# A decoder kernel: where the value projection's second weight block is fetched, where one accumulated pair is issued, and where the first keys are split

## The chip, the cores and the metric

The kernel runs on one core of a Trainium2 chip. The metric is the device time of one execution in microseconds. TensorE (PE in the profile) multiplies, ACT and DVE (ScalarE and VectorE) work on tiles in SBUF and PSUM, POOL (GpSimd) does small arithmetic and issues accumulating DMAs, and SP, ACT and POOL each issue DMAs on a queue of their own.

## What is computed

A two-layer decoder over 512 tokens of width 1024: a gated linear attention layer with its MLP, then a layer of stick-breaking attention with its MLP. Each mixer and each MLP is followed by a layer norm of the residual sum. The part that matters here is the seam between the layers:

```python
        h = layer_norm(DEEPNORM_ALPHA * h + sq_relu_mlp(h, mlp_w_up[layer], mlp_w_down[layer]),
                       ln_g[layer, 1], ln_b[layer, 1])
...
                kv = h @ kv_w
                k_sh = kv[..., :D].reshape(B, S, SB_HEADS, SB_HEAD_DIM)
                v_sh = kv[..., D:].reshape(B, S, SB_HEADS, SB_HEAD_DIM)
            q = (h @ sb_w_q[j]).reshape(B, S, SB_HEADS, SB_HEAD_DIM)
```

The norm of the first layer's MLP gives h (512 x 1024); keys, values and queries are products of h with 1024 x 1024 weights.

## The kernel before

**Numbers in two parts.** Every float32 operand of a product is split into a high part in float32r, which ACT copies (`hi`, L70 for weights, L98 for activations), and the remainder, which DVE subtracts (`lo`, L72 and L99). A product is three matmuls: hi by hi, hi by lo, lo by hi. Weights come in tiles of 128 x 1024 float32, 512 KB. A weight tile is fetched either through a pool of three tiles called `raw` on SP's queue (`split_piece`, L64), or into one of eight block tiles called `B`. The `hi` and `lo` tiles have pools of six. A tile of a pool is given out again in turn, and the instruction that fills it waits until the last reader of its former contents is done.

**Four token tiles.** h is held as four tiles of 128 tokens, 0 to 3. When the MLP has added its last product to a tile (DVE, L169), the two statistics instructions (L177) and their aggregate (L182) run on DVE, the factor on POOL (L183, L184), and DVE centres and scales the tile (L190). PE then turns the tile by eight 128 x 128 transposes (L231, a "turn"), ACT applies the norm's gain and bias while it copies out of PSUM (L234, into the tiles `s`), and L98 and L99 split the result into the tiles `T`: for each half u of the 1024 columns a hi (T_4181, T_4183) and a lo tile (T_4182, T_4184). `finish` (L245) does this as the MLP's last steps come; the turns of tiles 2 and 3 are left over as `late` and are called inside `values`.

**Values by seven products.** `values` (L768) computes V = h Wv by Strassen-Winograd's scheme on 2 x 2 blocks: the tokens split into tiles 0, 1 and 2, 3, the inner dimension into two halves, the columns of V into two halves. `v_weights(k, h, j)` is half h (256 rows) of weight block (k, j). Some operands are sums of weight blocks. These are formed in the block tiles, partly by accumulating DMAs on POOL's queue (`more`, L762), partly by DVE (L821, L822). `load` (L752) fetches plain blocks on ACT's queue (L758).

The order of PE's work in this stage is written out in `values`: the first product (`p1`, weights (0,0), plain) on tile 0; the turn of tile 2; the first product on tile 1; the second (`p2`, weights (1,0), plain) on tile 0; the turn of tile 3; the second on tile 1; the first pair's keys in two halves of 256 tokens (`cols_by`, 24 matmuls each), the first half of which needs only tiles 0 and 1; the first pair's queries (24 matmuls of 512 columns); then the fourth, fifth, sixth, third and seventh product. Each product is 24 matmuls of 512 columns (L794). The first and second product need only tiles 0 and 1.

Within an engine the instructions run in order, and that order is settled when the program is built: a scheduler places them by its own estimate of readiness, and `tc.keep_in_program_order` pins those that are given to it. A DMA that waits holds up what stands behind it in its engine's order; so does a split that waits for its weights.

The fetches of the stage before the change: `p1` and `p2` (four raw tiles), the keys' and queries' weights (one raw tile each) on SP's queue, in that order, so that with three raw tiles the second half of `p2` waits until the first half of `p1` is split. On ACT's queue `load` fetches blocks (1,1) and (0,1) when the norm of tile 0 begins, and (0,0) and (1,0) behind the turn of tile 1. On POOL's queue `more` adds (0,1) to the first and (0,0) to the second of these, two DMAs each, when the norm of tile 1 has begun (after `yield t` for t = 1).

## Time and profile before

| what | us |
|---|---|
| median of 3 runs | 1126.36 |
| lowest and highest | 1123.74 and 1127.30 |
| the profiled execution, whole | 1127.99 |
| its span, first to last instruction | 1126.3 |
| the stage that the change edits, on PE | 546.25 to 609.2 of the span |

The profile is of one execution, and its rows are times from the start of the span. The page cuts the span into 40 slices of 28.2 us; one of its rows is the clock that PE was granted, in tenths of full speed (9 is 90% or more):

```profile
PEclk9999999999999999999989999999999999999999
```

The one slice with an 8 begins at 563. The rows of the timeline show start and duration of an instruction (or of several alike, with their count), its engine, line and operation, the tiles it writes and reads, and in brackets how long the engine had been idle and what it waited for. Matmuls overlap in these rows, so their pace is read from the distance of their starts.

### The profile page before, as it was taken

The numbers are of one execution on the slowest core, as the hardware profiler recorded it, in microseconds if no ns is written. First come the engines' busy times: TensorE is split into PE (matmuls) and PEld (weight loads), VectorE is DVE, ScalarE is ACT, GpSimd is POOL, SyncE is SP. The second block draws the span as 40 slices with busy tenths as digits, with TensorE's granted clock in tenths as the row PEclk, the third lists the DMA queues.
The fourth block names the chain that finished last, engine by engine and source line by source line (L and its number), as shares of the span: only waits on it lengthen the run. The fifth ranks groups of instructions, "written<-read, shape, count | busy, mean of one in ns | idle before, by whom it ended". The sixth has DMA issues, their size and how long they took to land.

```text
span 1126.3 us, 14423 instructions
## 1 busy us (share of the span) xinstructions
PE 1111.5 (99%) x5515; PEld 920.9 (82%) x5515; DVE 828.5 (74%) x993; ACT 559.9 (50%) x839; POOL 175.0 (16%) x217
## 2 busy tenths in 40 slices
PE   9999999999999999999899999999999999999998
PEld 7888888898888888888778777788988888888886
DVE  4578649958957856849688898896479767667677
ACT  4455437643534533535565666654445435336353
POOL 1011222200100100121300335240100000000232
PEclk9999999999999999999989999999999999999999
DMA  7441399492670760877924321211946815816783
GB/s 242 126 131 56 120 248 210 130 302 77 203 208 19 204 187 23 228 180 163 247 58 125 100 89 62 76 38 38 273 139 180 253 54 150 223 38 183 176 135 87
DMA packets 108089, 162.78 MB, mean 145 GB/s; under 512 B 12466, under 2 KB 37426, under 8 KB 108020
## 3 DMA queue, kind: packets, MB, share of 16 engines
q1 hardware_dynamic: 86228, 119.39, 32.7%
q0 software_dynamic: 19328, 37.75, 19.4%
q10 hardware_dynamic: 2464, 4.72, 1.1%
q8 instruction: 43, 0.70, 0.2%
q14 instruction: 26, 0.21, 0.1%
HBM read 158.69 MB, written 3.15 MB: 144 GB/s over the span
## 4 chain that ended last, share of the span: by engine, by line
PE 95%; DVE 2%; DMA 1%; ACT 1%; issue 1%; POOL 0%; SPq 0%; POOLq 0%; ACTq 0%; DVEq 0%
PE ps L355 28%; PE ps L93 19%; PE ps L95 19%; PE ps L94 19%; PE ps L794 3%; PE ps L976 2%; PE ps L925 2%; PE ps L962 2%; PE ps L231 1%; DMA raw<-in_kv_w_dram 1%; DVE lo L72 1%; DMA h<-in_x_dram 0%; PE ps L584 0%; PE ps L121 0%; PE ps L649 0%
## 5 line engine op out<-in xcount | busy, mean ns | idle before, releaser
L355 PE MATMUL ps<-hi,T 128*128 128x512 f32 x1008 | 313.4, 390 | 0.1
L93 PE MATMUL ps<-T,hi 128*128 128x512 f32 (+1 forms) x776 | 291.7, 376 | 1.8 <-ACT hi L70 1.8
L95 PE MATMUL ps<-T,lo 128*128 128x512 f32 (+1 forms) x776 | 288.2, 371 | 0.9 <-DVE lo L72 0.9
L94 PE MATMUL ps<-T,hi 128*128 128x512 f32 (+1 forms) x776 | 288.2, 371 | 0.0
L72 DVE TENSOR_TENSOR lo<-raw,hi 128x1024 fp32r<-128x1024 f32 x132 | 160.8, 1223 | 97.5 <-ACT hi L70 93.9
L355 PEld LDWEIGHTS ps<-hi,T 128*128 128x128 f32 x1008 | 188.9, 188 | 40.0 <-DVE T L99 0.6
L70 ACT ACTIVATE hi<-raw 128x1024 fp32r<-128x1024 f32 x132 | 139.8, 1064 | 164.3 <-PE ps L94 53.5
L70 ACT ACTIVATE hi<-B 128x1024 fp32r<-128x1024 f32 x116 | 122.3, 1058 | 172.5 <-PE ps L94 103.8
L72 DVE TENSOR_TENSOR lo<-B,hi 128x1024 fp32r<-128x1024 f32 x116 | 140.4, 1220 | 85.4 <-ACT hi L70 85.2
L355 PE MATMUL ps<-lo,T 128*128 128x512 f32 x504 | 196.1, 389 | 0.0
L93 PEld LDWEIGHTS ps<-T,hi 128*128 128x128 f32 x776 | 147.6, 190 | 26.4 <-ACT hi L70 2.2
L95 PEld LDWEIGHTS ps<-T,lo 128*128 128x128 f32 x776 | 147.6, 190 | 26.2 <-DVE lo L72 1.2
L94 PEld LDWEIGHTS ps<-T,hi 128*128 128x128 f32 x776 | 147.6, 190 | 23.3
L314 POOL DMA_DIRECT2D B<-in_mlp_w_down_dram x52 | 62.9, 1257 | 543.9 <-DMA B<-in_mlp_w_down_dram 411.2
L355 PEld LDWEIGHTS ps<-lo,T 128*128 128x128 f32 x504 | 94.6, 188 | 19.6
L169 DVE TENSOR_TENSOR h<-h,ps 128x512 f32<-128x512 f32 x110 | 74.7, 681 | 6.9 <-PE ps L95 4.0
L93 PE MATMUL ps<-hi,T 128*128 128x512 f32 x192 | 77.4, 403 | 0.0
L95 PE MATMUL ps<-hi,T 128*128 128x512 f32 x192 | 75.3, 392 | 0.0
L94 PE MATMUL ps<-lo,T 128*128 128x512 f32 x192 | 75.1, 391 | 0.0
L99 DVE TENSOR_TENSOR T<-s,T 128x1024 fp32r<-128x1024 f32 (+1 forms) x50 | 53.4, 1070 | 20.8 <-ACT T L98 20.8
L952 DVE TENSOR_TENSOR_SCAN r<-r,begin 128x512 f32<-128x512 f32 x40 | 65.8, 1651 | 2.8 <-ACT r L949 2.8
L953 POOL TENSOR_TENSOR w<-w,r 128x512 f32<-128x512 f32 x32 | 52.2, 1632 | 94.3 <-DVE r L952 68.2
(190 smaller groups left out, 1246.0 us busy)
## 6 DMA issues: line engine op xcount, KB each, us to landing
raw<-in_mlp_w_up_dram SPq DMA_DIRECT2D x64, 512.0 KB, 5.8
B<-in_mlp_w_down_dram SPq DMA_DIRECT2D x64, 512.0 KB, 5.4
B<-in_mlp_w_down_dram POOLq DMA_DIRECT2D x52, 512.0 KB, 8.0
raw<-in_gla_w_in_dram SPq DMA_DIRECT2D x20, 512.0 KB, 3.7
raw<-in_mlp_w_down_dram SPq DMA_DIRECT2D x16, 512.0 KB, 4.5
B<-in_gla_w_o_dram POOLq DMA_DIRECT2D x14, 512.0 KB, 9.6
raw<-in_kv_w_dram SPq DMA_DIRECT2D x14, 512.0 KB, 5.2
B<-in_gla_w_o_dram SPq DMA_DIRECT2D x8, 512.0 KB, 6.1
```

The costliest lines, as they stand in the source:

```text
L70: nc.scalar.activation(hi, raw, AF.Copy)
L72: nc.vector.tensor_tensor(lo, raw, hi.bitcast(F32), op=ALU.subtract)
L93: keep(nc.tensor.matmul(ps, lhsT=a[0], rhs=b[0], start=first, stop=False))
L94: keep(nc.tensor.matmul(ps, lhsT=a[0], rhs=b[1], start=False, stop=False))
L95: keep(nc.tensor.matmul(ps, lhsT=a[1], rhs=b[0], start=False, stop=last))
L99: keep(nc.vector.tensor_tensor(lo, ps, hi.bitcast(F32), op=ALU.subtract))
L169: nc.vector.tensor_tensor(h, h, ps, op=op)
L314: nc.gpsimd.dma_start(out=b.rearrange("p (a b) -> p a b", a=2), in_=weights(k, h, j), accum_op=ALU.add)
L355: nc.tensor.matmul(banks[s], lhsT=a(k, s)[x], rhs=b[k][y], start=opens and (k, x, y) == (0, 0, 0), stop=closes and (k, x, y) == (3, 1, 0), ...
L794: nc.tensor.matmul(banks[s], lhsT=a(k, s)[x], rhs=b[k][w], start=opens and (k, x, w) == (0, 0, 0), stop=closes and (k, x, w) == (3, 1, 0), ...
L952: nc.vector.tensor_tensor_scan(down, down, begins[kind][:, ::-1], 1.0, op0=ALU.mult, op1=ALU.max)
L953: (nc.vector if kind == 2 else nc.gpsimd).tensor_tensor(w, w, r[:, 1:S + 1], op=ALU.mult)
```

## The change

- The first four block loads on ACT's queue are now (1,0) and (1,1) in place of (1,1) and (0,1); the later four are (0,0) and (0,1) in place of (0,0) and (1,0).
- The second product takes its weights from block (1,0) itself, split where it lies (`pieces(b21)`), in place of a plain fetch through two raw tiles. The same block later takes its sums and serves the fourth product, as before.
- POOL adds (0,1) to block (1,1) when the norm of tile 1 has begun, as before. Its other pair, now (0,0) added to block (0,1), is issued in `values`, behind the norms of tiles 2 and 3.
- The keys' weights are fetched and split (`piece_128`) in the code ahead of the turn of tile 3 in place of behind the second product.
- The splits of the fourth product's weights are pinned to program order.

```diff
-    def split_tile(raw, a):
+    def split_tile(raw, a, keep=lambda ins: ins):
...
-        nc.scalar.activation(hi, raw, AF.Copy)
+        keep(nc.scalar.activation(hi, raw, AF.Copy))
...
-        nc.vector.tensor_tensor(lo, raw, hi.bitcast(F32), op=ALU.subtract)
+        keep(nc.vector.tensor_tensor(lo, raw, hi.bitcast(F32), op=ALU.subtract))
...
-        b22, b12, b11, b21 = bs
-        p1, p2 = plain(0, 0), plain(1, 0)
+        b21, b22, b11, b12 = bs
+        p1, p2 = plain(0, 0), pieces(b21)
         part(0, whole(0, 0), p1, ys, True, False)
         late.pop(0)(None)
         part(1, whole(0, 0), p1, ys, True, False)
         part(0, whole(1, 0), p2, xs)
+        keys0 = piece_128(kv_w, 0)
         late.pop(0)(None)
         part(1, whole(1, 0), p2, xs)
-        keys0 = piece_128(kv_w, 0)
+        more(b12, 0, 0)
...
-        p4 = pieces(b21)
+        p4 = pieces(b21, tc.keep_in_program_order)
...
                 if t == 0:
-                    bs.extend(load(pool, k, j) for k, j in ((1, 1), (0, 1)))
+                    bs.extend(load(pool, k, j) for k, j in ((1, 0), (1, 1)))
                 yield t
+                if t == 1:
+                    more(bs[1], 0, 1)
                 if t == ~1:
-                    bs.extend(load(pool, k, j) for k, j in ((0, 0), (1, 0)))
-                if t == 1:
-                    more(bs[0], 0, 1)
-                    more(bs[1], 0, 0)
+                    bs.extend(load(pool, k, j) for k, j in ((0, 0), (0, 1)))
```

Three places in the engines' orders show what moves. The first is on ACT, at the end of the turn of tile 1. `hi_4611` of before and `hi_4605` of the change are the second half of the second product's weights; T_4181 is the hi of the turned tokens' first 512 columns. Before:

```order
L234 ACTIVATE s_4185<-ps_4530,bcol_4188,gcol_4187 128x128 x3
L70 ACTIVATE hi_4611<-raw_4609 128x1024
L98 ACTIVATE T_4181<-s_4185 128x4x128
L758 DMA B_4541<-in_kv_w_dram 128x2x512
L758 DMA B_4543<-in_kv_w_dram 128x2x512
```

And with the change:

```order
L234 ACTIVATE s_4185<-ps_4528,bcol_4188,gcol_4187 128x128 x3
L70 ACTIVATE hi_4605<-B_4429 128x1024
L98 ACTIVATE T_4181<-s_4185 128x4x128
L758 DMA B_4539<-in_kv_w_dram 128x2x512
L758 DMA B_4541<-in_kv_w_dram 128x2x512
```

The order is the same; what the split reads has moved from a raw tile to a block tile. The second place is on ACT too, from the end of the turn of tile 2 on. `hi_4713` of before and `hi_4672` of the change are the keys' weights, `hi_4769` and `hi_4765` the queries'. Before:

```order
L234 ACTIVATE s_4185<-ps_4639,bcol_4188,gcol_4187 128x128 x3
L234 ACTIVATE s_4186<-ps_4676,bcol_4188,gcol_4187 128x128
L98 ACTIVATE T_4181<-s_4185 128x4x128
L234 ACTIVATE s_4186<-ps_4676,bcol_4188,gcol_4187 128x128 x3
L234 ACTIVATE s_4185<-ps_4687,bcol_4188,gcol_4187 128x128
L98 ACTIVATE T_4183<-s_4186 128x4x128
L234 ACTIVATE s_4185<-ps_4687,bcol_4188,gcol_4187 128x128 x3
L70 ACTIVATE hi_4713<-raw_4711 128x1024
L98 ACTIVATE T_4181<-s_4185 128x4x128
L70 ACTIVATE hi_4769<-raw_4767 128x1024
L98 ACTIVATE T_4812<-s_4186 128x4x256
```

And with the change:

```order
L234 ACTIVATE s_4185<-ps_4633,bcol_4188,gcol_4187 128x128 x3
L70 ACTIVATE hi_4672<-raw_4670 128x1024
L98 ACTIVATE T_4181<-s_4185 128x4x128
L234 ACTIVATE s_4186<-ps_4676,bcol_4188,gcol_4187 128x128 x4
L234 ACTIVATE s_4185<-ps_4687,bcol_4188,gcol_4187 128x128
L98 ACTIVATE T_4183<-s_4186 128x4x128
L234 ACTIVATE s_4185<-ps_4687,bcol_4188,gcol_4187 128x128 x3
L70 ACTIVATE hi_4765<-raw_4763 128x1024
L98 ACTIVATE T_4181<-s_4185 128x4x128
L98 ACTIVATE T_4808<-s_4186 128x4x256
```

The keys' split has moved from behind the turn of tile 3 to the end of the turn of tile 2, and the queries' split stands one T further ahead, in the keys' old place. DVE's two subtractions (L72) move with them. The third place is on POOL, around the norms of tiles 2 and 3; ve and rs are their factors. One piece of the difference, - before and + with the change:

```order
 L184 TENSOR_TENSOR rs_4458<-ve_4457,mhalf 128x1
-L765 DMA B_4427<-in_kv_w_dram 128x2x512
-L765 DMA B_4429<-in_kv_w_dram 128x2x512
 L765 DMA B_4431<-in_kv_w_dram 128x2x512
 L765 DMA B_4433<-in_kv_w_dram 128x2x512
-L183 TENSOR_SCALAR ve_4564<-mv_4563 128x1
-L184 TENSOR_TENSOR rs_4565<-ve_4564,mhalf 128x1
-L183 TENSOR_SCALAR ve_4585<-mv_4584 128x1
-L184 TENSOR_TENSOR rs_4586<-ve_4585,mhalf 128x1
+L183 TENSOR_SCALAR ve_4562<-mv_4561 128x1
+L184 TENSOR_TENSOR rs_4563<-ve_4562,mhalf 128x1
+L183 TENSOR_SCALAR ve_4583<-mv_4582 128x1
+L184 TENSOR_TENSOR rs_4584<-ve_4583,mhalf 128x1
+L765 DMA B_4543<-in_kv_w_dram 128x2x512
+L765 DMA B_4545<-in_kv_w_dram 128x2x512
```

Of the four accumulating DMAs ahead of the norms of tiles 2 and 3 two remain, and the other pair stands behind them. On SP's queue the two fetches for the second product are gone, and the fetches behind them move up. On PE the order changes by one row: the first matmul of the queries stands behind the first matmul of the keys' second half.

## The prediction

> **What bounds the kernel now.** I read the page first, then what TensorE waits for, then the clock it was granted around those waits, and only then the engines it waited for.

> ```profile
> PE 1111.5 (99%) x5515; PEld 920.9 (82%) x5515; DVE 828.5 (74%) x993; ACT 559.9 (50%) x839; POOL 175.0 (16%) x217
> ```

> PE is busy for 99% of the span, so a change that leaves the matmuls alone can win only PE's idle time, and time in which PE is busy at a lower clock. The table of PE's waits (engine, line, what was waited for, total us, times, longest) says where the idle time is:

> ```profile
> PE ps L231 <- DVE h L190: 4.3, 2, 4.2
> PE ps L93 <- ACT hi L70: 1.8, 1, 1.8
> PE ps L95 <- DVE lo L72: 0.9, 1, 0.9
> ```

> PE's rows in order of time put all three into the stage that the change edits, between the last matmul of the layer's MLP and the fourth of the seven products:

> ```profile
> 546.25 0.39 PE L794 MATMUL ps<-hi,T 128*128 128x512 f32 x1
> 548.74 0.39 PE L794 MATMUL ps<-hi,T 128*128 128x512 f32 x1
> 553.32 1.60 PE L231 MATMUL ps<-ident,h 128*128 128x128 f32 x8 [4.19 <-DVE h L190]
> 561.36 1.04 PE L231 MATMUL ps<-ident,h 128*128 128x128 f32 x8
> 562.15 0.48 PE L794 MATMUL ps<-hi,T 128*128 128x512 f32 x1
> 566.93 0.38 PE L93 MATMUL ps<-T,hi 128*128 128x256 f32 x1 [1.80 <-ACT hi L70]
> 568.38 0.58 PE L95 MATMUL ps<-T,lo 128*128 128x256 f32 x1 [0.95 <-DVE lo L72]
> 574.40 0.28 PE L93 MATMUL ps<-T,hi 128*128 128x256 f32 x1
> 576.56 0.40 PE L93 MATMUL ps<-T,hi 128*128 128x512 f32 x1
> 582.03 0.39 PE L794 MATMUL ps<-hi,T 128*128 128x512 f32 x1
> ...
> 582.19 27.20 PE ps L794 x120
> ```

> What the stage would take without waits follows from its own undisturbed rows: 120 matmuls of 512 columns take 27.20, so 0.227 each; eight transposes take 562.15 - 561.36 = 0.79; the 18 of 256 columns from 574.40 to 576.56 take 0.12 each; the 24 of the queries run from 576.56 to 582.03, 5.47. The stage has 48 at 0.227 (10.9), two turns (1.6), 48 at 0.12 (5.8) and 5.5, which is 23.7 us. It takes 582.03 - 546.25 = 35.8. So **12.1 us** are lost, and only 6.9 of them are the three waits. The granted clock shows where the rest is (stretch, its length, PE busy and count, clock, DMA share, GB/s):

> ```profile
> 546.93:550.35 3.42, 2.20 (x10) 1.00 1.11 212
> 550.35:553.76 3.41, 0.44 (x4) 1.00 1.12 215
> 553.76:557.17 3.41, 3.41 (x12) 0.50 1.09 276
> ...
> 564.00:567.41 3.41, 1.61 (x7) 1.00 0.23 61
> 567.41:570.83 3.42, 2.47 (x12) 0.50 0.61 123
> 570.83:574.24 3.41, 3.41 (x18) 0.50 0.64 190
> 574.24:577.65 3.41, 3.41 (x26) 1.00 0.01 2
> ```

> After the stretch with 0.44 busy the clock is half for 3.41; after the one with 1.61 busy it is half for 6.83. Half of the first is 1.7, half of the second without its 0.95 of idle is 2.9: 4.6 us are slow clock, and the remaining half microsecond is pipelines that drain and fill.

> **The first wait.** ACT, then DVE, then POOL:

> ```profile
> 540.73 8.83 DMA raw<-in_kv_w_dram
> ...
> 544.85 1.22 ACT L234 ACTIVATE s<-ps,bcol,gcol 128x128 f32<-128x128 f32 x3
> 549.64 1.06 ACT L70 ACTIVATE hi<-raw 128x1024 fp32r<-128x1024 f32 x1 [3.58 <-DMA raw<-in_kv_w_dram]
> 550.61 0.61 ACT L98 ACTIVATE T<-s 128x512 fp32r<-128x512 f32 x1
> ...
> 547.80 0.20 DVE L182 BATCH_NORM_AGGREGATE mv<-bst 128x2 f32<-128x12 f32 x1
> 551.25 0.69 DVE L99 TENSOR_TENSOR T<-s,T 128x512 fp32r<-128x512 f32 x1 [3.25 <-ACT T L98]
> 551.86 0.69 DVE L177 BATCH_NORM_STATS2 bst<-h 128x6 f32<-128x512 f32 x1
> 552.46 0.80 DVE L190 TENSOR_SCALAR h<-h,mv,rs 128x1024 f32<-128x1024 f32 x1
> ...
> 548.11 0.22 POOL L183 TENSOR_SCALAR ve<-mv 128x1 f32<-128x1 f32 x1 [4.46 <-DVE mv L182]
> 548.40 0.57 POOL L184 TENSOR_TENSOR rs<-ve,mhalf 128x1 f32<-128x1 f32 x1
> 553.47 1.08 POOL L183 TENSOR_SCALAR ve<-mv 128x1 f32<-128x1 f32 x1 [4.50 <-DVE mv L182]
> ```

> The second half of the second product's weights could be fetched only when the first raw tile came free (540.73), and landed after 8.83. ACT stood 3.58 before its split (L70); behind that in ACT's order stands L98 of tile 1, DVE's L99 waits for that, and behind L99 in DVE's order stand the statistics and the centring (L190) that tile 2's transposes need. POOL had tile 2's factor ready at 548.97.

> **The change, part by part.** (1) The blocks (1,0) are now the first two of the four loads that ACT's queue issues ahead of the turns. The first two of before landed in 5.2 us and the slowest of all eight in 11.1 (the last fence below), so they are there by 542, and ACT comes to the second split at 546.1 (544.85 + 1.22). Then L70 (1.06) and L98 (0.61) end at 547.7, DVE does L99, L177 and L190 from 548.0 on: 0.69 + 0.69 + 0.80, a little overlapped, 550.0. If L183 is held by DVE's L99, as it was held to 1.08 at 553.47, the factor comes at 549.3 and L190 ends at 550.1. I take 550.1. PE would have gone on at 548.97 (548.74 + 0.23), so of the first loss **1.1 us stays**; what is late next is the chain L99, L177, L190 itself. Bounds: 0.9 if all overlap, 2.0 if L183 takes 1.08 and pushes L190 to 551.

> (2) The first keys' weights take the third raw tile and need no release from the second product; their split stands between the turns on ACT and DVE, ahead of PE's need: PE turns tile 2 at 550.1, does 24 matmuls (5.4) to 556.3, turns tile 3, and reaches the keys at 559.9. The split is over when ACT and DVE have finished turn 2, at about 556. The waits of 1.80 and 0.95 go. What is late next is tile 3's own split: from its transposes to the end of its last L99 before the change is 561.36 to 568.93 by these rows, with one L98 of tile 2 in the way that is then long done:

> ```profile
> 568.25 0.68 DVE L99 TENSOR_TENSOR T<-s,T 128x512 fp32r<-128x512 f32 x1
> ...
> 576.26 1.22 DVE L72 TENSOR_TENSOR lo<-B,hi 128x1024 fp32r<-128x1024 f32 x1
> ```

> 7.6 less 0.5 from 556.3 is 563.4; the second half of the keys, which reads tile 3, wants it at 563.05 (559.9 + 24 x 0.12 and two matmuls). **0.4 us** of wait; bounds 0 and 1. The queries' first matmul, which now stands inside the second half of the keys, wants only the queries' hi; ACT makes it ahead of that last L98, and its fetch starts when the first raw tile comes free (540.73), so even at 19.6 it has landed by 560.4, when ACT gets there.

> (3) The fourth product's weights now follow at once: DVE's first lo began 8.0 us after the start of the last L99 (576.26 and 568.25). One lo (1.22) that stood between stands ahead of L99 now, so it begins 6.9 after 562.7 and is over at 570.8; PE wants it at 571.7. Nothing is added, but the cover is 0.9 us where it was 4.6.

> (4) The pair of accumulated loads for block (0,1) goes behind the last norm on POOL. The two norms that it passes win nothing, since POOL stood idle 4.46 ahead of the first of them. Behind the pair stand only the MEMSETs of the attention stage's masks, so nothing of this stage is delayed on that engine; the wait is for the landing.

> ```profile
> 538.69 4.96 POOL L765 DMA_DIRECT2D B<-in_kv_w_dram  x4
> ...
> DMA to landing us min/median/max: 7.5/12.4/17.4
> ...
> DMA to landing us min/median/max: 5.2/7.3/11.1
> ...
> B<-in_kv_w_dram ACTq DMA_DIRECT2D x2, 512.0 KB, 5.2
> ...
> raw<-in_sb_w_q_dram SPq DMA_DIRECT2D x1, 512.0 KB, 19.6
> ```

> The first row is POOL's four issues of before, 1.24 each. The other rows give the time from issue to landing: of POOL's four accumulated loads, of all eight of ACT's, of ACT's first two, and of the queries' weights. ACT issues the plain loads at about 548 to 549.5, they land by 553 to 560.6, POOL adds its 1.24 an issue, and the pair has landed at about 569 to 571 by the median. The fifth product begins at 571.5 + 5.4 = 576.9 and its split takes 1.06 and 1.22, so the pair is wanted by 574.6: some 4 us of cover.

> (5) Two fetches of 512 KB and their SPq issues are removed, so the stage moves 16 blocks and pieces in place of 18, and SP's later fetches are issued earlier. The number of matmuls, splits and adds is the same.

> **Sum.** Lost before 12.1; left 1.1 + 0.4 + 0.1 for a drained pipeline: gain 10.5 us. No stretch is left with less than two thirds of its time busy, and the stretch with 2.20 of 3.42 kept its clock. The profiled execution took 1127.99, and so 1117.5. It stands 1.63 above the median of the three runs (1126.36); part of that may be slow clock, which the change takes away in any case, part an offset, and I halve it: **1116.7 us**, 0.9% less than the median.

> [...]

> **Rivals.** First, **a wait takes the place of the first one**: POOL's L183 held by DVE's L99 and then the next instruction, as at 553.47, so that tile 2 is late by 2.0 and with it less than half of a stretch is busy: 0.9 more of idle and 1.7 of slow clock, 1119.3. For it: L183 took 1.08 beside DVE work. Against: L99 is only 0.69 long. 11%.

> Second, **the second slow stretch isn't made by those waits**, and PE runs it at half clock though it waits for nothing: 2.9 more, 1119.6. For it: PE was not idle for a whole stretch before it. Against: the page's clock row, shown above, falls in one slice of forty, the one that begins at 563, and nowhere that PE works without waits. 5%. [...]

> Third, **no change to speak of**: the new pair lands late. At 17.4 after the latest issue (563.1) it lands at 580.5, 5.9 too late, and a slow stretch (1.7) follows: 7.6 of the 10.5 are given back, 1124.3. Or the blocks of the second product land late as well; they would have to take over 15 us, where 11.1 is the longest of ACT's. 8%.

> Fourth, **slower**: the pair stands in ACT's and DVE's order ahead of the sixth product's splits, so if it lands after about 583 the wait and the slow clock behind it eat all of the gain, and at 588 the kernel takes 1131.8. That is 25 us after POOL's issue or more; the longest landing in this stretch, in a DMA jam that now has two transfers less, is 19.6. 4%.

> **How the numbers follow.** The forecast has 72%, with 1114.5 to 1118.5 as its own range (all of the 12.1 at the lower end, an unlucky 1 to 2 us at the upper). With the first two rivals that is 88%, and the range is 1114 to 1121. Three runs of this kernel spread over 0.3%, about what a measurement can tell from no change: faster by more than that means below 1123. Faster 0.88, same 0.08, slower 0.04.

> **What would show it.** Right: PE's wait for L190 at about 549 falls from 4.2 to near 1, the waits for L70 and L72 are gone, the granted clock is 1.00 in every stretch of the stage, and the fourth product starts some 25 us after the first in place of 35.8. Step 1 is wrong if ACT's second split still waits for a DMA; step 2 if PE waits for L99 before the second half of the keys by more than 1; step 3 if it waits for L72 before the fourth product; step 4 if ACT waits for block (0,1). The prediction as a whole is wrong if the slow clock stays without its waits.

## The result and the profile after

The changed kernel takes 1117.21 us (median of 4 runs, 1116.37 to 1117.43), beside 1125.11 for the kernel before in the same comparison; the ratio is 0.9927, with a 95% interval of 0.9907 to 0.9947. The forecast was 1116.7. The profiled execution took 1117.43 with a span of 1115.7, where that of before took 1127.99 and 1126.3.

From the page of the changed kernel, the busy times and the granted clock by slices:

```profile
PE 1106.8 (99%) x5515; PEld 917.2 (82%) x5515; DVE 828.4 (74%) x993; ACT 559.7 (50%) x839; POOL 175.1 (16%) x217
PEclk9999999999999999999999999999999999999999
```

The number of instructions is the same, PE's busy time is 4.7 us less (1111.5 before), and the slice with an 8 is gone. Half of the busy time in the three stretches of before at a clock of 0.50 is 4.6 us, and in the changed kernel each of the seven stretches from 546.82 to 570.69 is at 1.00: by these numbers the busy time that went was slow clock. What PE waits for in the changed kernel (engine, line, what was waited for, total us, times, longest):

```profile
...
PE ps L231 <- DVE h L190: 1.2, 2, 1.0
...
```

The waits of 1.8 for L70 and of 0.9 for L72 are gone and that for L190 has fallen from 4.3 to 1.2; the two rows left out lie in other stages. PE's rows of the stage in order of time (start, duration, in brackets the idle time ahead), with the row of the chain that holds the rest of the products:

```profile
545.92 0.39 PE L794 MATMUL ps<-hi,T 128*128 128x512 f32 x1
548.41 0.39 PE L794 MATMUL ps<-hi,T 128*128 128x512 f32 x1
549.83 1.09 PE L231 MATMUL ps<-ident,h 128*128 128x128 f32 x8 [1.03 <-DVE h L190]
556.24 1.03 PE L231 MATMUL ps<-ident,h 128*128 128x128 f32 x8
559.85 0.28 PE L93 MATMUL ps<-T,hi 128*128 128x256 f32 x1
562.72 0.51 PE L93 MATMUL ps<-T,hi 128*128 128x256 f32 x2
563.35 0.39 PE L94 MATMUL ps<-T,hi 128*128 128x256 f32 x1
571.44 0.39 PE L794 MATMUL ps<-hi,T 128*128 128x512 f32 x1
...
573.03 0.39 PE L794 MATMUL ps<-lo,T 128*128 128x512 f32 x1
...
571.60 27.20 PE ps L794 x120
```

From the first product to the fourth it is 571.44 - 545.92 = 25.5 us, 35.8 before: the stage gives 10.3 of the 10.6 by which the span is shorter; the other 0.3 lies ahead of it, since its first product starts at 545.92 in place of 546.25. In between only two gaps are left: 1.03 ahead of tile 2's transposes, and some 0.3 in the second half of the keys. (Of the two matmuls at 562.72 one is the keys', of 256 columns, and one the queries' first, of 512; at 0.12 and 0.23 the matmul at 563.35 would stand at 563.07.)

The stretches of the stage on the same measure as before (PE, PEld, DVE, ACT and POOL busy and count, clock, DMA share, GB/s):

```profile
546.82:550.23 3.41, 2.38 (x13) 1.71 (x12) 3.25 (x8) 0.35 (x1) 1.35 (x3) 1.00 1.08 297
...
560.46:563.87 3.41, 3.29 (x27) 2.98 (x26) 3.41 (x4) 3.23 (x5) 0.00 (x0) 1.00 1.07 169
```

These two are the stretches with a gap; neither has less than 2.38 us of work, and the clock is 1.00 in both. On ACT, DVE and POOL, what stands ahead of tile 2's transposes:

```profile
545.51 1.15 ACT L70 ACTIVATE hi<-B 128x1024 fp32r<-128x1024 f32 x1
546.46 0.71 ACT L98 ACTIVATE T<-s 128x512 fp32r<-128x512 f32 x1
546.85 0.67 DVE L169 TENSOR_TENSOR h<-h,ps 128x512 f32<-128x512 f32 x1
547.44 0.20 DVE L182 BATCH_NORM_AGGREGATE mv<-bst 128x2 f32<-128x12 f32 x1
547.56 0.64 DVE L99 TENSOR_TENSOR T<-s,T 128x512 fp32r<-128x512 f32 x1
547.75 0.54 POOL L183 TENSOR_SCALAR ve<-mv 128x1 f32<-128x1 f32 x1 [6.92 <-DVE mv L182]
548.12 0.69 DVE L177 BATCH_NORM_STATS2 bst<-h 128x6 f32<-128x512 f32 x1
548.36 0.57 POOL L184 TENSOR_TENSOR rs<-ve,mhalf 128x1 f32<-128x1 f32 x1
548.97 0.81 DVE L190 TENSOR_SCALAR h<-h,mv,rs 128x1024 f32<-128x1024 f32 x1 [0.16 <-POOL rs L184]
...
549.82 1.17 DVE L72 TENSOR_TENSOR lo<-B,hi 128x1024 fp32r<-128x1024 f32 x1
549.98 1.08 POOL L183 TENSOR_SCALAR ve<-mv 128x1 f32<-128x1 f32 x1 [1.05 <-DVE mv L182]
```

ACT's second split reads a block tile (`hi<-B`) and follows the work ahead of it without a wait, where before it stood 3.58 for its DMA. DVE then works through L169, L182, L99, L177 and L190 with one gap of 0.16. The first wait is now a chain of computation, not a landing.

### The profile page after: what moved, and what is told of

Same layout as the page of the kernel before. It is cut to its first block, busy times and chain, and to the rows that moved or that the text cites. A ratio compares the mean times of both kernels' runs of the same rounds, so it can differ in the third digit from the quotient of the medians.

```text
span 1115.7 us, 14408 instructions
## 1 busy us (share of the span) xinstructions
PE 1106.8 (99%) x5515; PEld 917.2 (82%) x5515; DVE 828.4 (74%) x993; ACT 559.7 (50%) x839; POOL 175.1 (16%) x217
## 4 chain that ended last, share of the span: by engine, by line
PE 96%; DVE 2%; issue 1%; POOL 0%; ACT 0%; POOLq 0%; DVEq 0%; ACTq 0%
PE ps L355 29%; PE ps L93 19%; PE ps L94 19%; PE ps L95 19%; PE ps L794 3%; PE ps L976 2%; PE ps L925 2%; PE ps L962 2%; PE ps L231 1%; DVE lo L72 1%; PE ps L584 0%; DVE h L169 0%; PE ps L121 0%; DVE bst L177 0%; DVE T L99 0%
## 5 line engine op out<-in xcount | busy, mean ns | idle before, releaser
L93 PE MATMUL ps<-T,hi 128*128 128x512 f32 (+1 forms) x776 | 290.3, 374 | 0.0
L95 PE MATMUL ps<-T,lo 128*128 128x512 f32 (+1 forms) x776 | 287.0, 370 | 0.0
L72 DVE TENSOR_TENSOR lo<-raw,hi 128x1024 fp32r<-128x1024 f32 x130 | 158.5, 1224 | 98.5 <-ACT hi L70 94.8
L70 ACT ACTIVATE hi<-raw 128x1024 fp32r<-128x1024 f32 x130 | 137.8, 1064 | 163.2 <-PE ps L355 58.8
L70 ACT ACTIVATE hi<-B 128x1024 fp32r<-128x1024 f32 x118 | 124.4, 1059 | 169.7 <-PE ps L94 104.0
L72 DVE TENSOR_TENSOR lo<-B,hi 128x1024 fp32r<-128x1024 f32 x118 | 142.9, 1221 | 83.9 <-ACT hi L70 83.8
L95 PEld LDWEIGHTS ps<-T,lo 128*128 128x128 f32 x776 | 146.3, 189 | 25.0
L93 PEld LDWEIGHTS ps<-T,hi 128*128 128x128 f32 x776 | 146.2, 189 | 24.3 <-issue 0.7
L169 DVE TENSOR_TENSOR h<-h,ps 128x512 f32<-128x512 f32 x110 | 74.8, 682 | 6.9 <-PE ps L95 4.0
L93 PE MATMUL ps<-hi,T 128*128 128x512 f32 x192 | 77.4, 403 | 0.0
L95 PE MATMUL ps<-hi,T 128*128 128x512 f32 x192 | 75.3, 392 | 0.0
L99 DVE TENSOR_TENSOR T<-s,T 128x1024 fp32r<-128x1024 f32 (+1 forms) x50 | 53.4, 1069 | 10.6 <-ACT T L98 10.6
## 6 DMA issues: line engine op xcount, KB each, us to landing
raw<-in_mlp_w_up_dram SPq DMA_DIRECT2D x64, 512.0 KB, 5.6
B<-in_mlp_w_down_dram SPq DMA_DIRECT2D x64, 512.0 KB, 5.3
B<-in_mlp_w_down_dram POOLq DMA_DIRECT2D x52, 512.0 KB, 8.0
raw<-in_gla_w_in_dram SPq DMA_DIRECT2D x20, 512.0 KB, 3.6
raw<-in_mlp_w_down_dram SPq DMA_DIRECT2D x16, 512.0 KB, 4.4
B<-in_gla_w_o_dram POOLq DMA_DIRECT2D x14, 512.0 KB, 8.5
raw<-in_kv_w_dram SPq DMA_DIRECT2D x12, 512.0 KB, 4.5
B<-in_gla_w_o_dram SPq DMA_DIRECT2D x8, 512.0 KB, 6.2
```

Of the source, the lines that this page charges most:

```text
L70: keep(nc.scalar.activation(hi, raw, AF.Copy))
L72: keep(nc.vector.tensor_tensor(lo, raw, hi.bitcast(F32), op=ALU.subtract))
L93: keep(nc.tensor.matmul(ps, lhsT=a[0], rhs=b[0], start=first, stop=False))
L95: keep(nc.tensor.matmul(ps, lhsT=a[1], rhs=b[0], start=False, stop=last))
L99: keep(nc.vector.tensor_tensor(lo, ps, hi.bitcast(F32), op=ALU.subtract))
L169: nc.vector.tensor_tensor(h, h, ps, op=op)
```

## The experiments

**One part at a time.** In the first kernel the keys' split goes back behind the second product and the other edits stay; in the second, the kernel before gets only the earlier keys.

```diff
         part(0, whole(1, 0), p2, xs)
-        keys0 = piece_128(kv_w, 0)
         late.pop(0)(None)
         part(1, whole(1, 0), p2, xs)
+        keys0 = piece_128(kv_w, 0)
         more(b12, 0, 0)
```

> The change without its third part: the keys' split stands behind the second product again. Theory (the parts end different waits): PE's wait for L190 stays near 1.0 us as in the changed kernel, the two waits in front of the keys come back at about 1.8 and 0.95 us, and a stretch of half clock follows them in the executions in which one of them fills half of a stretch: 1120 to 1123 us, 3 to 6 above the changed kernel. Rival (the second loss was only an echo of the first, a clock or a DMA queue still disturbed): no wait in front of the keys, 1117 to 1118.

Measured 1122.39 (1120.09 to 1123.2, 9 runs), ratio 0.9957 (0.9943 to 0.9971). What PE waits for in this kernel:

```profile
PE ps L93 <- ACT hi L70: 1.8, 1, 1.8
...
PE ps L231 <- DVE h L190: 1.2, 2, 1.0
PE ps L95 <- DVE lo L72: 0.9, 1, 0.9
```

As the theory had it, the blocks alone bring the wait for L190 to the 1.2 of the changed kernel and leave the keys' two waits at the sizes of before. Eight of the nine executions have a mean clock of 0.998 or less; the ninth, at 1.0, is the fastest (1120.09).

```diff
         part(0, whole(1, 0), p2, xs)
+        keys0 = piece_128(kv_w, 0)
         late.pop(0)(None)
         part(1, whole(1, 0), p2, xs)
-        keys0 = piece_128(kv_w, 0)
```

> The kernel before with only the keys' split moved ahead of the turn of tile 3. Theory: the wait of 4.2 us for L190 and its slow clock stay; the waits of 1.8 and 0.95 go, though the keys' weights land late here (their raw tile comes free at 542.5 and such a fetch took up to 18 us), so that ACT stands at their split before it turns tile 3 and some 1 us of wait comes back in the keys' second half: 1120 to 1123 us. Rival (the split only moves the stall to ACT, and the last tile is as late as before): 1125 to 1127.

Measured 1122.69 (1122.27 to 1123.59, 10 runs), ratio 0.9964 (0.995 to 0.9977). The waits, and ACT's splits in order of time:

```profile
PE ps L231 <- DVE h L190: 5.6, 2, 5.4
```

```profile
550.05 1.06 ACT L70 ACTIVATE hi<-raw 128x1024 fp32r<-128x1024 f32 x1 [4.87 <-DMA raw<-in_kv_w_dram]
...
560.45 1.06 ACT L70 ACTIVATE hi<-raw 128x1024 fp32r<-128x1024 f32 x1 [2.15 <-DMA raw<-in_kv_w_dram]
```

Here the keys' waits are gone, and ACT still stands at the second product's split (4.87), so PE's first wait stays, at 5.4. The wait of some 1 us that was expected back in the keys' second half did not come. Against the 1126.6 of before in this comparison the two parts alone gain 4.2 and 3.9 us, together 8.1. The whole gained 7.9 in its own comparison (1125.11 to 1117.21) and 9.8 in a later one (1126.70 to 1116.87, below). So the parts about add up; whether there is more when both are there can't be told from these. Each part needs its own edit, and neither is a by-product of the other.

**The pair ahead of the norms.** The pair is put back behind the turn of tile 1, ahead of the factors of tiles 2 and 3 on POOL. The order of ACT and DVE shifts with it: they take the keys' and the queries' splits before the turn of tile 2.

```diff
-                nc.gpsimd.tensor_scalar(ve, mv[:, 1:2], LN_EPS, None, op0=ALU.add)
-                nc.gpsimd.tensor_tensor(rs, ve, mhalf[:, 0:1], op=ALU.pow)
+                tc.keep_in_program_order(nc.gpsimd.tensor_scalar(ve, mv[:, 1:2], LN_EPS, None, op0=ALU.add))
+                tc.keep_in_program_order(nc.gpsimd.tensor_tensor(rs, ve, mhalf[:, 0:1], op=ALU.pow))
...
-        more(b12, 0, 0)
...
                     bs.extend(load(pool, k, j) for k, j in ((0, 0), (0, 1)))
+                    more(bs[3], 0, 0)
```

> The changed kernel with the pair for block (0,1) ahead of the norms of tiles 2 and 3 on POOL. Theory (the pair is harmless only because it stands behind them): POOL waits with the pair until its block has landed, about 555.8, issues for 2.5 us, and tile 2's factor comes some 10 us late; PE idles about 10 us before turn 2 and runs at half clock behind that: 1128 to 1133 us. Rival (POOL's queue has slack, the place is free): 1117 to 1119.

Measured 1130.66 (1129.31 to 1131.96, 8 runs), ratio 1.0033 (1.0016 to 1.005), so 13 us slower than the change. From its timeline, POOL, DVE and PE:

```profile
555.28 1.20 POOL L765 DMA_DIRECT2D B<-in_kv_w_dram  x1 [14.84 <-DMA B<-in_kv_w_dram]
...
558.56 0.72 POOL L183 TENSOR_SCALAR ve<-mv 128x1 f32<-128x1 f32 x1
...
559.96 0.81 DVE L190 TENSOR_SCALAR h<-h,mv,rs 128x1024 f32<-128x1024 f32 x1 [6.53 <-POOL rs L184]
...
560.83 1.97 PE L231 MATMUL ps<-ident,h 128*128 128x128 f32 x8 [12.45 <-DVE h L190]
```

POOL stands 14.84 us and issues the accumulating load only when the plain load of its block has landed (555.28), and with the new order of the blocks this block is among the last four. The factor of tile 2, 0.72 and 0.57 us of work, stands behind it, and PE waits 12.45. So the new order of the blocks can't do without the pair's new place. In the order of before that move alone would win nothing by the traces, since POOL stood idle there ahead of tile 2's factor (4.46); it wasn't run. The pin on the fourth product's splits, by contrast, leaves every engine's order as it is without it.

**The order without the earlier fetch.** The kernel before, with the turn of tile 1 ahead of the second product's second split on ACT; what is fetched, and into which tiles, stays as it was. Other orders move with it: DVE centres tile 2 ahead of L99 of tile 1, PE does two of the first product's twelve matmuls on tile 0 ahead of the turn of tile 2 in place of all twelve, the keys' split stands ahead of the turn of tile 3, and ACT issues its block loads from 546.12 on in place of 549.69.

```diff
-                turn_affine(sp, u, t, hs[t].h[:, 512 * u:512 * u + 512], cols, y)
+                with tc.high_priority() if room and t == 1 else ExitStack():
+                    turn_affine(sp, u, t, hs[t].h[:, 512 * u:512 * u + 512], cols, y)
```

> The kernel before, fetches as they were, with the turn of tile 1 given precedence, so that ACT splits the second product's second half behind L98 of tile 1 and DVE centres tile 2 ahead of L99 of tile 1 (the scheduler also moves the keys' split ahead of turn 3). Theory (the first wait is a matter of ACT's and DVE's order, the fetch only fills it): the wait for L190 falls below 1 us with the same late fetch; but the keys' weights, which land at 555 to 561 here, hold ACT, and a wait of 1 to 4 us comes back at the keys with slow clock behind it: 1118 to 1124. Rival (the missing weights themselves hold PE): PE waits as long as before, now for the second product's hi or lo: 1124 to 1127.

Measured 1124.38 (1122.86 to 1126.22, 10 runs), ratio 0.998 (0.9965 to 0.9996), 2.2 us under before: on the time alone this decides little. The trace does. PE's waits of this kernel, and from its timeline the centring and the turn of tile 2 and ACT's waits for weights:

```profile
PE ps L231 <- DVE h L190: 2.2, 3, 1.7
...
PE ps L93 <- ACT T L98: 1.1, 1, 1.1
PE ps L94 <- DVE T L99: 0.9, 1, 0.9
PE ps L95 <- DVE lo L72: 0.8, 1, 0.8
PE ps L93 <- ACT hi L70: 0.5, 1, 0.5
```

```profile
548.31 0.81 DVE L190 TENSOR_SCALAR h<-h,mv,rs 128x1024 f32<-128x1024 f32 x1 [0.39 <-POOL rs L184]
...
549.18 1.59 PE L231 MATMUL ps<-ident,h 128*128 128x128 f32 x8 [1.70 <-DVE h L190]
...
549.45 1.06 ACT L70 ACTIVATE hi<-raw 128x1024 fp32r<-128x1024 f32 x1 [2.76 <-DMA raw<-in_kv_w_dram]
...
562.70 1.06 ACT L70 ACTIVATE hi<-raw 128x1024 fp32r<-128x1024 f32 x1 [8.88 <-DMA raw<-in_kv_w_dram]
```

With nothing of tile 1 behind the waiting split, tile 2 is centred at 549.12 (548.31 + 0.81), 4.1 us ahead of before (552.46 + 0.80), though ACT's split still waits 2.76 for the same fetch. So it was the place of that split in the orders of ACT and DVE, not the landing as such, that held tile 2. PE's wait falls only from 4.2 to 1.7, where less than 1 was expected, because PE itself comes to the turn earlier: at 547.48 (549.18 - 1.70), 549.13 before. The next fetch, the keys', makes ACT stand 8.88, and behind that split stands tile 3: four later waits, 3.3 us in all, take back most of it. In the changed kernel neither wait for a fetch is left.

**A late factor.** To measure what lateness of tile 2 costs, two, four or six multiplications of one column by 1 are put on POOL between L183 and L184 for tile 2.

```diff
                 nc.gpsimd.tensor_scalar(ve, mv[:, 1:2], LN_EPS, None, op0=ALU.add)
+                for _ in range(extra):
+                    nc.gpsimd.tensor_scalar(ve, ve, 1.0, None, op0=ALU.mult)
                 nc.gpsimd.tensor_tensor(rs, ve, mhalf[:, 0:1], op=ALU.pow)
...
-                hs[t].stats()
+                hs[t].stats(2 if room and t == 2 else 0)
```

> The changed kernel with two more multiplications by 1 on POOL between L183 and L184 of tile 2, which delay its factor by about 0.6 us and change no other engine's order. PE idles about 1.6 us before turn 2. Theory (the clock falls after a stretch of 3.41 us that is about half idle or more, with edges that do not follow the program): clock kept, 1117.8 us. Rival (any idle above 1.2 us takes the clock): 1119.5. [...]

> The same with four multiplications, about 1.2 us: PE idles about 2.2 us in one piece. Theory: the clock falls in some executions (when 1.8 us or more of the idle lie in one stretch) and not in others: 1118.4 without, about 1120.1 with, so runs that differ by 1.7. [...]

> The same with six multiplications, about 1.8 us: PE idles about 2.8 us in one piece. Theory: the clock falls in most executions, 1119.0 without and 1120.7 to 1121.4 with. [...]

| multiplications | longest wait for the centring, us | median of 4, us | executions that lost clock |
|---|---|---|---|
| 0 (the change) | 1.03 | 1117.21 | 0 |
| 2 | 1.38 | 1117.74 | 0 |
| 4 | 2.27 | 1118.35 | 0 |
| 6 | 2.80 | 1120.17 | 3 |

Up to 2.27 the time follows the wait one for one (1.24 us of wait for 1.14 of time, the first row being from the first comparison). At 2.80 three of four executions run at a mean clock of 0.998 or less and take 1.0 to 1.7 more than the fourth (1118.96). Whether 2.27 can cost clock was open, and the last two kernels were run again, in more executions:

> The changed kernel with the factor of tile 2 late by four multiplications (as in e5_late4, where PE stood idle for 2.3 us in one piece and the clock stayed at full in all four executions). Theory as the prediction has it (a 3.41 us window that is idle for 1.8 us or more takes the clock down; where the windows begin is random in each execution): an idle piece of 2.27 us is cut by a window's edge into two pieces below 1.8 in 1.33 of 3.41 cases, so the clock falls in about 6 executions of 10, and those take 1.7 us longer (1120.1 against 1118.4). Rival: the window must be idle for longer than 2.27 us in one piece, so it falls in none of them, and all stay between 1118.0 and 1118.8.

> The same with six multiplications, idle for 2.8 us in one piece. Theory: cut into two pieces below 1.8 in 0.79 of 3.41 cases, so the clock falls in 7 or 8 executions of 10 (1120.0 to 1120.7), and 2 or 3 stay at 1119.0. Rival (2.27 us is never enough, so a window needs at least 2.3 us of idle): the piece lies in one window with 2.3 or more in (3.41 - 2.3 + 0.5) of 3.41 cases at most, so it falls in 5 of 10 or fewer. [...]

Four multiplications: 1119.26 (1118.12 to 1120.56, 6 runs), three of six at 0.998 or less (1119.39, 1120.01, 1120.56). Six: 1120.03 (1118.97 to 1121.74, 6 runs), four of six. With the first runs that is 3 of 10 and 7 of 10, where the theory has about 6 and 7 or 8 (an estimate from 1.8 us of idle time in one stretch, which is 3.41 less the 1.61 of before, and from edges taken to fall anywhere). So few executions can't tell 6 from 3, nor 7 from the 5 of the rival; what they settle is that an idle piece of about 2.3 us can be enough: it stood at 2.25 in the trace in which half clock followed. The piece differs a little between executions: in the traces of these two runs it is 2.25 and 2.53 where it was 2.27 and 2.80. Stretches that end where the clock changed, of the second kernel with four multiplications:

```profile
548.73:552.14 3.41, 1.16 (x10) 1.13 (x10) 2.07 (x4) 0.43 (x2) 2.11 (x5) 1.00 1.05 382
552.14:555.55 3.41, 3.41 (x9) 2.64 (x8) 1.53 (x3) 3.41 (x10) 0.70 (x3) 0.50 0.88 342
```

of the first with six:

```profile
549.41:552.82 3.41, 1.31 (x10) 1.27 (x11) 2.02 (x3) 0.61 (x2) 2.07 (x4) 1.00 1.06 405
552.82:556.23 3.41, 3.41 (x10) 2.69 (x9) 1.50 (x2) 3.41 (x9) 1.29 (x2) 0.51 0.66 255
```

and of the kernel with the order changed and no earlier fetch, in rows of 3.41 counted from its one slow stretch:

```profile
546.23:549.64 3.41, 1.43 (x8) 0.76 (x7) 3.02 (x7) 0.65 (x2) 1.09 (x3) 1.00 1.09 232
549.64:553.05 3.41, 3.41 (x12) 2.92 (x11) 2.64 (x5) 3.41 (x9) 0.81 (x2) 0.50 1.10 271
...
566.69:570.10 3.41, 1.88 (x13) 1.36 (x11) 3.05 (x4) 3.41 (x7) 0.00 (x0) 1.00 0.68 126
570.10:573.51 3.41, 2.87 (x24) 2.87 (x25) 3.41 (x4) 0.87 (x2) 0.00 (x0) 1.00 0.57 159
```

**What is left, taken away.** In the changed kernel DVE does the last adds of the MLP (L169) behind splits of weights. Here they go ahead of those.

```diff
-                nc.vector.tensor_tensor(h, h, ps, op=op)
+                with tc.high_priority() if last and hurry else ExitStack():
+                    nc.vector.tensor_tensor(h, h, ps, op=op)
```

`hurry` is set only while the first layer's last norm is built.

> The changed kernel with precedence for the last add (L169) of each tile at the end of the first layer's MLP, so that DVE adds, aggregates and centres tile 2 ahead of the splits and of L99 of tile 1. Theory (the 1.0 us that is left is the chain of L99, L177 and L190 on DVE): the wait for L190 falls below 0.3 and the time by 0.7 to 1.2, to about 1116.2. Rival (POOL's factor or PE's own last product sets the turn): the wait stays at 0.8 or more, 1117.2; or the splits that are put off hold the first or second product: 1118.

Measured 1115.77 (1115.62 to 1116.77, 4 runs), ratio 0.9901 (0.9886 to 0.9916). It and the change were then run beside each other on one chip:

> The changed kernel itself, for a comparison on one chip with f4_add_first_again: 1117.2 if the first comparison holds (1116.4 to 1117.4), clock 0.999 or more in every execution. If the spread of the kernel before (1123.6 to 1131.6) is made by where the clock's windows begin against its waits, this kernel, whose longest idle piece is 1.03 us, spreads by less than 1.5 us.

> The changed kernel with the adds at the end of the MLP ahead of the splits on DVE (as in e9_add_first: 1115.77). Theory: the wait for L190, 1.2 us in the changed kernel, is the only time left in the stage, and this kernel is 1.0 to 1.6 us faster than f3_after_again on the same chip. Rival: the gain of the first comparison was one of chip, and the two differ by less than 0.5 us.

The change took 1116.87 (1116.48 to 1119.73, 6 runs), ratio 0.9919 (0.99 to 0.9937); the adds ahead 1115.48 (1115.2 to 1116.01, 5 runs), ratio 0.9901 (0.9883 to 0.992), and so 1.4 us less. PE's wait for the centring in the latter:

```profile
...
PE ps L234 <- DVE h L193: 0.2, 1, 0.2
```

The wait for the centring (L193 in this kernel) is 0.2 in place of 1.2, and this version beats both kernels. Its first product starts at 545.55 and its fourth at 569.55: the stage takes 24.0 us, 1.5 less than with the change and 0.3 above the 23.7 without waits. The expected spread of the change, under 1.5 us, was missed: two of its six executions took 1118.26 and 1119.73, at a mean clock of 0.999. The profile is of another execution, so what they lost stays open.

## Why the prediction was right

- **The bound.** Right. 12.1 us lost were read from the stage; it now loses 25.5 - 23.7 = 1.8, so 10.3 came back, where 10.5 were expected.
- **(1) The blocks.** Right: the turn of tile 2 at 549.83 where 550.1 was expected (the stage starts 0.33 earlier in this trace), a wait of 1.03 for 1.1, and what is late next is the chain on DVE that was named; the kernel with the adds ahead shows it, since the wait goes when that chain starts earlier. L183 took 0.54 beside L99 in place of 0.22, but not 1.08. The kernel with the order changed and no earlier fetch shows the other half of the argument, that the orders of ACT and DVE carried the wait to tile 2.
- **(2) The keys.** Right: both waits are gone, the keys start at 559.85 (559.9), and the wait for tile 3's last L99 is 0.3, where the sum has 0.4. The sum counted the queries' matmul there like one of the keys'; at its own 0.23 the second half wants tile 3 at 563.13, and the wait expected is 0.3 as well.
- **(3) The fourth product's weights.** Right, and near the margin named (0.9), for the first of the two tiles; the second was not looked at. From the timeline of the changed kernel:

```profile
569.48 1.22 DVE L72 TENSOR_TENSOR lo<-B,hi 128x1024 fp32r<-128x1024 f32 x1
...
571.22 3.50 DVE L72 TENSOR_TENSOR lo<-B,hi 128x1024 fp32r<-128x1024 f32 x3
```

The first lo is over at 570.70 (570.8 expected), 0.74 ahead of the fourth product's first matmul at 571.44. That matmul reads the hi; the first that reads this lo starts one matmul later, at 571.67. The second lo is the first of the three at 571.22 and is over at 572.44; the matmul that reads it starts at 573.03. Its cover of 0.59 is thinner still.

- **(4) The pair.** Right in effect, a little too cautious in time. The two issues, and the times from issue to landing of POOL's four accumulated loads:

```profile
555.80 2.49 POOL L765 DMA_DIRECT2D B<-in_kv_w_dram  x2 [4.09 <-ACT T L98]
...
DMA to landing us min/median/max: 7.2/8.8/10.4
```

The second begins at about 557.0 (555.80 + half of 2.49) and has landed by 567.4 at the latest; 569 to 571 was expected, with landings of 12.4 and up to 17.4. ACT, which splits the block from about 570.6 on, doesn't wait for it. The expected range was narrower than its own terms: plain loads at 553 to 560.6, 1.24 an issue and 12.4 to land give 566.6 to 575.5, and the late end lies behind the 574.6 at which the pair was wanted, so the 4 us of cover were no bound. The longest landing is 7 us shorter, in a stage with two fetches less. That the pair's place matters at all was missed: "the two norms that it passes win nothing" is true of the order of before, but with the new order of the blocks they would lose 12.45 us behind it.

- **(5) Two fetches less.** Part of (1) and (4); not tried alone.
- **The sum.** The profiled executions agree to 0.1: 1117.43 for 1117.5. That close it is partly luck: the stage gave 10.3 where 10.5 were expected, and 0.3 came from its earlier start, which no term foresaw. No run shows the term of 0.1 for a drained pipeline, nor that the half microsecond of before was pipelines that drain and fill; both are the author's estimates. Of the 1.8 that the stage now loses, the two gaps are 1.03 and some 0.3, and what the other 0.5 is was not shown. The one term that was mis-sized is the offset: 0.8 us, half of the 1.63 by which the profiled execution of before stood above its median, was taken off, but the profiled execution after stands only 0.22 above its own median. So nearly all of the 1.63 looks like slow clock, which the change takes away and which the sum had already counted. The spread of before bears this out: in the first experiments' comparison the executions of before at a mean clock of 0.998 or more took 1123.6 to 1126.7, and those at 0.995 or less 1126.5 to 1131.6; its profiled one stood at 0.994.
- **The rivals.** None came. The first, tile 2 late by 2.0 for 1119.3, has its price measured: a wait of about 2.3 gives 1118.1 to 1119.1 where the clock holds, and 1119.4 to 1120.6 in the 3 of 10 executions where it falls. The second is out, since the clock is 1.00 in all seven stretches from 546.82 to 570.69 once the waits are gone. The third and fourth needed a late pair, and the landings went the other way; the experiment that put the pair ahead of the norms shows how the change could have been slower, on POOL's order rather than by the landing itself.
- **The clock.** The prediction's first rival reckons with slow clock where less than half of a stretch is busy. Seven stretches now bear on it: half clock follows 0.44, 0.88, 1.16, 1.31, 1.43 and 1.61 us of work in 3.41, full clock follows 1.88. They agree with it, half of 3.41 being 1.7; where between 1.61 and 1.88 the clock stops falling was not shown.

## What to carry to other kernels

Here a split that waited 3.58 us for its weights delayed what stood behind it in ACT's and DVE's orders, and PE waited 4.19, so look there, and not only at who reads the weights, when PE waits for something that was computed in time elsewhere. Price a wait with the clock that it costs: here 6.9 us of waits brought 4.6 of slow clock with them, and with the waits down to 1.3 the clock was 1.00 in all seven stretches. When the order of the loads is changed, follow every queue on which an instruction waits for one of them; in the kernel that put two tiny norm instructions (0.72 and 0.57 us) behind an accumulating load on POOL, PE waited 12.45 us for them.

## What was not expected of the hardware

- Whether a wait costs clock differs from one execution to the next: an idle piece of about 2.3 us did so in 3 of 10, one of 2.5 to 2.8 in 7 of 10. The edges of the clock's stretches differed between two executions: with six multiplications the slow stretch begins at 552.82 in one trace and at 551.29 in the other. That a piece which an edge cuts in two goes free is the author's explanation and was not shown, since the edges can be read only where the clock changes.
- A one-column instruction on POOL ended with the DVE instruction beside it: L183 took 0.54 and ended 0.09 us after L99, and 1.08 beside an L72 that ended 0.07 us before it, where with DVE idle beside it, it took 0.22 (at 548.11 before the change). Whether DVE held it was not shown: no run was made for it.
- The accumulated loads landed in 8.8 us by the median where they took 12.4 before, with two transfers of 512 KB less in the stage. How much of that is the two transfers, and how much the later issue of the pair, wasn't tried.
